# A feed forward in seven block products instead of eight, with its inner layer and the residual held in DRAM

## The chip, the core and the metric

The kernel runs on one core of one Trainium2 chip. The core has TensorE (PE) for matmuls, VectorE (DVE), ScalarE (ACT) and GpSimd (POOL) for element-wise work, and DMA queues that are fed in order by SyncE (SP) and a few other engines. The metric is the device time of one execution in microseconds, as the median of several runs.

## The reference

One decoder block on 1024 tokens of width 1024. What comes ahead of the feed forward (state-space and attention mixers, a gated merge, cross attention to 256 memory tokens) is left as it is. The last lines of the reference are these:

```
xo = memory_cross_attention(h, mem, w_xq[l], w_xkv[l], w_xo[l])
h = layer_norm(DEEPNORM_ALPHA * h + xo, ln2_g[l], ln2_b[l])

ff = jnp.square(jax.nn.relu(h @ w_ff1[l] + b_ff1[l])) @ w_ff2[l] + b_ff2[l]
h = layer_norm(DEEPNORM_ALPHA * h + ff, ln3_g[l], ln3_b[l])
```

The feed forward is 1024 x 1024 by 1024 x 4096, a squared ReLU, and 1024 x 4096 by 4096 x 1024.

## The kernel before

Every float32 product is made of three matmuls on rounded operands: each operand is split into a high part (a cast on ScalarE) and a low part (a subtraction on VectorE), and `mm3` (lines 99 to 102) sums high x high, high x low and low x high in one PSUM bank. A matmul covers 128 contraction rows, 128 stationary columns and 512 moving columns.

**Weights** come through the class `Stream` (lines 105 to 161). `load` starts a DMA on SP's queue into one of two raw buffers, `split` makes the two parts in one of `NWH` = 6 tile pairs (lines 136 and 137), `done` frees a pair. `pump` does one load and one split at each `slot()` (line 272); `slot` also runs deferred work (`defer`, line 269), whose count is in slots. All engines run their own instructions in the order in which the program writes them.

**The cross attention's last product** is a call of `nat_gemm` (line 1234 on) with `evac_xo` (lines 1324 to 1329): for each of two column halves it runs over eight token tiles `t` of 128; the last two tiles share their weight steps. After the second half, every pair of tiles gets its layer norm (`ln_pair`, line 1258 on): statistics on VectorE, the reciprocal root by small steps on GpSimd (`ln_rstd`, lines 212 to 233), the centering on VectorE (line 241), the scaling on ScalarE (line 250), the bias on GpSimd (line 252). Three slots later `tail_xo` transposes the tile on TensorE (line 262) and splits it into `xh` and `xl` (lines 255 and 256), which are the moving operand of the feed forward.

**The feed forward** (lines 1333 to 1397) goes over eight groups `hc` of 512 inner columns. For each it makes 2 halves of the tokens x 4 inner blocks x 8 contraction blocks x 3 matmuls (up), applies ReLU on ScalarE (line 1349), the square on GpSimd (1350), the split on ScalarE and VectorE (1351, 1352) into `fh`, `fl`; and then 8 token tiles x 2 column halves x 4 contraction blocks x 3 matmuls (down), whose PSUM result VectorE adds into the residual `hn` (line 1368). The inner layer stays in SBUF and never leaves it. In the last group the order is by token tile, so that the final layer norm of a pair can begin while later tiles are multiplied (lines 1369 to 1396); the last two tiles are normalized one by one on VectorE, and the last store follows line 1395. Other names that the change touches: `open_pool("ptp")`, the pools of temporaries `sgp` and `rows`, the layout of `wff2` in `_layout` (line 1458).

Of the kernel before, what the change touches and what calls it, by code (L numbers as in the profile page):

```python
# [10 lines left out]
FT = mybir.dt.float32  # L11
# [47 lines left out]
def block_kernel(ctx, tc, I, out, dbg=None):  # L59
# [45 lines left out]
    class Stream:  # L105
        def __init__(self):
            self.req = []
            self.key = {}
            self.nd = self.ns = self.nu = 0
            self.raw = {}  # L110
            self.sp = {}
            self.over = set()
            self.nstart = 0

# [4 lines left out]
        def load(self, limit=10 ** 9):  # L119
            while self.nd < min(len(self.req), limit) and self.nd - self.ns < (3 if self.nd < self.nstart else 2):  # L120
                ap, n = self.req[self.nd]
                if self.nd < self.nstart and self.nd % 3 == 2:
                    t = kvp.tile([128, 1024], FT, name="wrx", tag="wrx", bufs=1)
                else:
                    t = win.tile([128, 1024], FT, name="wraw", tag="wraw", bufs=2)
                sp.dma_start(t[:, :n], ap)
                self.raw[self.nd] = t
                self.nd += 1

        def split(self, limit=10 ** 9):  # L130
            while self.ns < min(self.nd, limit) and (self.ns < NWH or self.ns - NWH in self.over):
                n = self.req[self.ns][1]
# [3 lines left out]
                act.copy(h[:, :n], r[:, :n])  # L136
                dve.tensor_sub(l[:, :n], r[:, :n], h[:, :n].bitcast(FT))  # L137
# [18 lines left out]
        def done(self, key=None):  # L156
            i = self.nu if key is None else self.key[key]
# [12 lines left out]
    g_dr = dr.tile([16, 128, SEQ], FT, name="g_dr")  # L170

# [31 lines left out]
    for hc in range(8):  # L203
        for i in range(4):
            W.add(I["wff1"][4 * hc + i], 1024)
        for i in range(4):
            W.add(I["wff2"][4 * hc + i], 1024)

# [81 lines left out]
    hh = actp.tile([128, KB, SEQ], FR, name="acth", tag="acth")  # L290
    hl = actp.tile([128, KB, SEQ], FR, name="actl", tag="actl")
# [884 lines left out]
    mx_c, mx = open_pool("mx", "right")  # L1176
    xh = actp.tile([128, KB, SEQ], FR, name="acth", tag="acth")
    xl = actp.tile([128, KB, SEQ], FR, name="actl", tag="actl")
# [48 lines left out]
    def nat_gemm(ah, al, evac):  # L1227
        for c in range(2):
            for ts_ in [(t,) for t in range(NT - 2)] + [(NT - 2, NT - 1)]:
                ws = [[w.rearrange("p (k c) -> p k c", k=2) for w in W.get(i)] for i in range(4)]  # L1230
                ps_ = [mmbank() for _ in ts_]
                for i in range(4):
# [5 lines left out]
                    if len(ts_) > 1:  # L1238
                        W.done()
                        slot() if i == 1 else W.pump()  # L1240
# [3 lines left out]

    rows_c, rows = open_pool("rows", "right")
# [37 lines left out]
    ptp_c, ptp = open_pool("ptp", "right")  # L1283
    ph = ptp.tile([128, 4, SEQ], FR, name="ph")
    pl = ptp.tile([128, 4, SEQ], FR, name="pl")

    def evac_xs(c, t, p):
        pp = (sgp if t % 2 else ptp).tile([128, 512], FT, name="sg", tag="sg", bufs=2)
# [31 lines left out]

    def tail_xo(t):
        transpose_in(hn[:, t, :], xh, xl, t)

    def evac_xo(c, t, p):
# [3 lines left out]
        if c == 1 and t % 2:  # L1328
            ln_pair(t, g2_, b2_, tail_xo, 3, 3)

    nat_gemm(Cat(ph, xh), Cat(pl, xl), evac_xo)

# [1 line left out]
    fh, fl = ph, pl  # L1334
    for t in range(NT):
        defer(t, lambda t=t: dve.scalar_tensor_tensor(hn[:, t, :], hn[:, t, :], ALPHA, bf2, op0=OP.mult, op1=OP.add))
    for hc in range(8):
        if hc == 7:
            g3, b3 = load_rows("ln3_g", "ln3_b")
        for half in range(2):  # L1340
            s = slice(512 * half, 512 * half + 512)
            for i in range(4):
                w = [t.rearrange("p (k c) -> p k c", k=KB) for t in W.get(0 if half else i)]
                p = mmbank()
                for k in range(KB):
                    mm3(p, w[0][:, k, :], w[1][:, k, :], xh[:, k, s], xl[:, k, s], k == 0, k == KB - 1)
                r = sgp.tile([128, 512], FT, name="sg", tag="sg", bufs=2)
                j = COL_F1 + 4 * hc + i
                act.activation(r, p, AF.Relu, bias=cols[:, j:j + 1], scale=1.0)  # L1349
                pool.tensor_mul(r, r, r)  # L1350
                act.copy(fh[:, i, s], r)  # L1351
                dve.tensor_sub(fl[:, i, s], r, fh[:, i, s].bitcast(FT))  # L1352
                if half:
                    W.done()
                slot()
        last = hc == 7
        for c, t in [(c, t) for t in range(NT) for c in range(2)] if last else [(c, t) for c in range(2) for t in range(NT)]:
            cs = slice(512 * c, 512 * c + 512)
            p = mmbank()
            sl = slice(128 * t, 128 * t + 128)  # L1360
            ws = [[w.rearrange("p (k c) -> p k c", k=2) for w in W.get(2 * c * last + i)] for i in range(2)]
            for k in range(4):
                w = ws[k // 2]
                mm3(p, fh[:, k, sl], fl[:, k, sl], w[0][:, k % 2, :], w[1][:, k % 2, :], k == 0, k == 3)
                if t == NT - 1 and k % 2 and not last:
                    W.done()
                    W.pump()
            dve.tensor_add(hn[:, t, cs], hn[:, t, cs], p)  # L1368
            if last:
                x = hn[:, t, :]  # L1370
                ln_stats(lnst[:, t], x, (c,))
                def cen(h):
                    xx, gg = x[:, 512 * h:512 * h + 512], g3[:, 512 * h:512 * h + 512]
                    return lambda mv: dve.scalar_tensor_tensor(xx, xx, mv[:, 0, 0:1], gg, op0=OP.subtract, op1=OP.mult)

                if c == 1 and t % 2 and t < NT - 2:
                    xs = [hn[:, u, :] for u in (t - 1, t)]
                    w = ln_a(xs, [lnst[:, u] for u in (t - 1, t)], g3)

                    def fin(t=t, xs=xs, w=w):  # L1380
                        ln_b(xs, w, b3, (pool, pool))
                        for u, x in zip((t - 1, t), xs):
                            sp.dma_start(out[128 * u:128 * u + 128, :], x)

                    defer(1, fin)
                elif c == 1 and t == NT - 2:
                    mv, w = ln_rstd([lnst[:, t]], dve, [cen(0), cen(1)])
                    act.activation(x, x, AF.Copy, scale=w[:, 1, 0:1])
# [105 lines left out]
```

## Time and profile before

| | |
|---|---|
| median of 3 runs | 1945.02 us (1944.44 to 1945.78) |
| span of the profiled execution | 1943.7 us |
| feed forward, first to last matmul | 1221.0 to 1927.0 us of the span |
| PE, DVE, ACT, POOL busy | 97%, 50%, 29%, 31% of the span |
| mean granted TensorE clock | 0.990 |

The span runs from the first to the last instruction of one profiled execution; the times of the runs are a little longer. A busy TensorE is not by itself TensorE at its peak, since matmuls overlap: one record lasts 0.39 us, but the next starts 0.226 us after it. So stages are read by counts of matmuls in a stretch rather than by the sum of durations.

### The profile page before, as it was taken

How to read it: one execution, taken by the hardware profiler on the slowest of the kernel's cores; microseconds unless marked ns; L12 is line 12 of the kernel's file. 1: busy time of each engine (PE TensorE's matmuls, PEld its weight loads, DVE VectorE, ACT ScalarE, POOL GpSimd, SP SyncE). 2: the span in 40 equal slices, each digit the busy share in tenths (PEclk: the TensorE clock that was granted, in tenths of full speed). 3: DMA queues.
4: the chain of work that ended last, by engine and by line, in shares of the span. 5: the costliest groups of instructions: out<-in, count | busy, mean ns of one | idle time of the engine just before them, and what ended most of it. 6: DMA issues, size and time to landing. Idle time of an engine off the chain costs nothing.

```text
span 1943.7 us, 24170 instructions
## 1 busy us (share of the span) xinstructions
PE 1885.0 (97%) x9400; PEld 1619.6 (83%) x9400; DVE 966.7 (50%) x1678; ACT 563.7 (29%) x998; POOL 609.0 (31%) x782
## 2 busy tenths in 40 slices
PE   7899999999999998999999999999999999999996
PEld 7798788889999976788888888788888888888885
DVE  6526846675666666444556445542323223232328
ACT  4324343433332434322124322412121212213121
POOL 3305687474565335322034004401010100101016
PEclk9999999999999999999999999999999999999998
DMA  6545562130120243333511121111111111011102
GB/s 243 184 122 187 183 198 73 34 99 23 55 67 29 75 136 109 118 117 109 185 44 44 44 76 44 44 65 44 55 54 44 44 44 66 32 55 48 62 21 87
DMA packets 82563, 163.26 MB, mean 84 GB/s; under 512 B 19857, under 2 KB 39441, under 8 KB 82449
## 3 DMA queue, kind: packets, MB, share of 16 engines
q1 hardware_dynamic: 75968, 147.30, 22.8%
q10 hardware_dynamic: 5904, 12.85, 1.7%
q0 software_dynamic: 576, 1.57, 0.3%
q8 instruction: 74, 1.21, 0.3%
q14 instruction: 41, 0.33, 0.1%
HBM read 126.99 MB, written 34.70 MB: 83 GB/s over the span
## 4 chain that ended last, share of the span: by engine, by line
PE 86%; DVE 7%; ACT 2%; issue 2%; POOL 2%; DMA 1%; DVEq 0%; SPq 0%; ACTq 0%; POOLq 0%
PE mm L100 26%; PE mm L102 26%; PE mm L101 26%; PE ax L262 1%; DVE wlo L137 1%; PE ax L996 1%; PE ax L969 1%; PE ax L987 1%; PE ax L822 1%; ACT yh L1111 1%; PE ax L845 1%; PE ax L954 1%; PE ax L809 1%; DVE lnst L237 0%; PE ax L846 0%
## 5 line engine op out<-in xcount | busy, mean ns | idle before, releaser
L100 PE MATMUL mm<-acth,whi 128*128 128x512 f32 (+1 forms) x896 | 348.0, 388 | 4.9 <-ACT abst L611 4.6
L102 PE MATMUL mm<-acth,wlo 128*128 128x512 f32 (+1 forms) x896 | 345.5, 386 | 2.5 <-DVE wlo L137 2.5
L101 PE MATMUL mm<-actl,whi 128*128 128x512 f32 (+1 forms) x896 | 345.4, 386 | 0.3 <-DVE actl L256 0.3
L136 ACT CAST whi<-wraw 128x1024 fp32r<-128x1024 f32 (+1 forms) x169 | 168.4, 996 | 419.5 <-PE mm L102 300.9
L137 DVE TENSOR_TENSOR wlo<-wraw,whi 128x1024 fp32r<-128x1024 f32 (+1 forms) x169 | 213.2, 1263 | 146.9 <-ACT whi L136 144.6
L100 PE MATMUL mm<-whi,acth 128*128 128x512 f32 (+1 forms) x704 | 281.7, 400 | 0.0
L102 PE MATMUL mm<-whi,actl 128*128 128x512 f32 (+1 forms) x704 | 270.7, 384 | 0.0
L101 PE MATMUL mm<-wlo,acth 128*128 128x512 f32 (+1 forms) x704 | 270.4, 384 | 0.0
L1350 POOL TENSOR_TENSOR sg<-sg 128x512 f32<-128x512 f32 x64 | 67.8, 1059 | 574.4 <-ACT sg L1349 574.4
L100 PE MATMUL mm<-whi,ph 128*128 128x512 f32 x576 | 224.3, 389 | 0.0
L102 PE MATMUL mm<-whi,pl 128*128 128x512 f32 x576 | 224.1, 389 | 0.0
L101 PE MATMUL mm<-wlo,ph 128*128 128x512 f32 x576 | 224.1, 389 | 0.0
L100 PEld LDWEIGHTS mm<-acth,whi 128*128 128x128 f32 x896 | 171.1, 191 | 38.4 <-ACT abst L611 5.5
L102 PEld LDWEIGHTS mm<-acth,wlo 128*128 128x128 f32 x896 | 170.6, 190 | 36.4 <-DVE wlo L137 3.0
L101 PEld LDWEIGHTS mm<-actl,whi 128*128 128x128 f32 x896 | 171.1, 191 | 32.6 <-DVE actl L256 0.5
L102 PEld LDWEIGHTS mm<-whi,actl 128*128 128x128 f32 x704 | 168.0, 239 | 15.3
L101 PEld LDWEIGHTS mm<-wlo,acth 128*128 128x128 f32 x704 | 168.6, 239 | 14.2
L100 PEld LDWEIGHTS mm<-whi,acth 128*128 128x128 f32 x704 | 167.5, 238 | 15.4
L1352 DVE TENSOR_TENSOR pl<-sg,ph 128x512 fp32r<-128x512 f32 x64 | 44.3, 692 | 261.8 <-ACT ph L1351 261.8
L1368 DVE TENSOR_TENSOR hn<-hn,mm 128x512 f32<-128x512 f32 x128 | 87.0, 685 | 163.7 <-PE mm L102 163.7
L102 PEld LDWEIGHTS mm<-whi,pl 128*128 128x128 f32 x576 | 108.1, 188 | 22.4
L101 PEld LDWEIGHTS mm<-wlo,ph 128*128 128x128 f32 x576 | 108.1, 188 | 22.4
(322 smaller groups left out, 2882.6 us busy)
## 6 DMA issues: line engine op xcount, KB each, us to landing
wraw<-in_wff_dram SPq DMA_DIRECT2D x64, 512.0 KB
wraw<-in_wg_dram SPq DMA_DIRECT2D x16, 512.0 KB
gl<-g_dr SPq DMA_DIRECT2D x32, 256.0 KB
wraw<-in_wqk_dram SPq DMA_DIRECT2D x12, 512.0 KB
wraw<-in_wglu_dram SPq DMA_DIRECT2D x16, 384.0 KB
g_dr<-abst SPq DMA_DIRECT2D x16, 256.0 KB
a_dr<-abst ACTq DMA_DIRECT2D x16, 256.0 KB
b_dr<-abst ACTq DMA_DIRECT2D x16, 256.0 KB
```

Source lines behind the costliest of these rows:

```text
L100: pe.matmul(o, lhsT=lh, rhs=rh, start=first, stop=False)
L101: pe.matmul(o, lhsT=lh, rhs=rl, start=False, stop=False)
L102: pe.matmul(o, lhsT=ll, rhs=rh, start=False, stop=last)
L136: act.copy(h[:, :n], r[:, :n])
L137: dve.tensor_sub(l[:, :n], r[:, :n], h[:, :n].bitcast(FT))
L262: pe.transpose(p[:, k, :], x[:, (4 * b + k) * 128:(4 * b + k + 1) * 128], ident)
L809: pe.matmul(p[:, g, :], lhsT=xe[:, g].rearrange("p j o -> p (j o)"), rhs=d["cm"][:, g, 0:8, :].rearrange("p j o -> p (j o)"), start=True, ...
L822: pe.matmul(p[:, g, :], lhsT=d["bt"][:, g, :], rhs=d["U"][:, g, :], start=True, stop=True)
L845: pe.matmul(p[:, g, :], lhsT=dts[:, g, :], rhs=d["U"][:, g, :], start=True, stop=False)
L1350: pool.tensor_mul(r, r, r)
L1352: dve.tensor_sub(fl[:, i, s], r, fh[:, i, s].bitcast(FT))
L1368: dve.tensor_add(hn[:, t, cs], hn[:, t, cs], p)
```

## The change

The whole feed forward is replaced. Both products are cut into 2 x 2 blocks (tokens 0 to 511 and 512 to 1023; contraction halves; column pairs), and each 2 x 2 block product is made from seven block products of sums and differences instead of eight plain ones.

- **Operands from the activations.** The tails of the cross attention's layer norm (`tail_lo`, `tail_hi`) make, besides the transposed blocks, three combined blocks S1, S2 and A11 - A21, and later S4 (`s4h`, `s4l`). `keep_residual` stores alpha * h + bias to a DRAM tensor `h2_dr`. The last two token tiles are normalized singly on VectorE.
- **Operands from the weights.** `operand` casts and subtracts one block for a product and then forms the next difference in place on GpSimd. For the up product it fills half of a stream tile (`f1_fill`), for the down product a whole 2048-column pair (`f2_weights`).
- **The up product** goes over 16 steps `j` of two inner blocks; `f1_step` combines the seven PSUM results on VectorE into four blocks, applies ReLU and square on ScalarE, forms sums and differences on GpSimd and stores seven tiles to `f_dr` in DRAM by SP's queue.
- **The down product** goes over four blocks `c` of 1024 inner columns and seven products each; the stationary operands are read back from `f_dr` by the weight stream, the residual from `h2_dr`. Products "1" and "6" are collected in `a1` and `a6` and added to the output by GpSimd in the last block; results "5" and "7" are added twice, once by VectorE and once through ScalarE and GpSimd. The final layer norm follows inside the last block (`last_pair`, `last_one`).

Cut to its core:

```
+    def tail_hi(t):
+        u = t - 4
+        cs = slice(128 * u, 128 * u + 128)
+        ct = slice(512 + 128 * u, 640 + 128 * u)
+        p = turned(t)
+        a11, a12 = flat(hn[:, u, 0:512]), flat(hn[:, u, 512:1024])
+        sa, s1 = flat(tmp(0)), flat(tmp(1))
+        act.copy(sa, p[0])
+        dve.tensor_add(s1, p[1], sa)
+        s2 = flat(tmp(0))
+        pool.tensor_sub(s2, s1, a11)
+        split_ps(xh[:, 0:4, ct], xl[:, 0:4, ct], s1)
+        split_ps(xh[:, 4:8, ct], xl[:, 4:8, ct], p[1])
+        pool.tensor_sub(sa, a11, sa)
+        split_ps(ph[:, :, cs], pl[:, :, cs], s2)
+        pool.tensor_sub(a12, a12, s2)
+        split_ps(ph[:, :, ct], pl[:, :, ct], sa)
+        keep_residual(t)
...
+    def operand(q, b11, b21, b12, b22, h, l):
+        src = {"1": b11, "2": b21, "3": b22, "4": b21, "5": b11, "6": b22, "7": b12}[q]
+        act.copy(h, src)
+        dve.tensor_sub(l, src, h.bitcast(FT))
+        if q == "1":
+            pool.tensor_sub(b11, b12, b11)
+        elif q == "3":
+            pool.tensor_sub(b12, b22, b12)
+            pool.tensor_sub(b22, b22, b11)
+        elif q == "6":
+            pool.tensor_sub(b21, b21, b22)
...
+    f1_seq = [(j, q) for j in range(16) for q in ("1267543" if j < 15 else "1567243")]
...
+    t_free = [(ph[:, :, 0:512], pl[:, :, 0:512]), (ph[:, :, 512:], pl[:, :, 512:]),
+              (quad(xh, 1, 0), quad(xl, 1, 0)), (quad(xh, 1, 1), quad(xl, 1, 1))]
+    f2_order = ["1", "2", "6", "5", "3", "7", "4"]
+    f2_made = ["1", "2", "3", "6", "5", "7", "4"]
...
+        if q == "1":
+            act.copy(u, p)
+        elif q == "2":
+            dve.tensor_add(x11, u, p)
+            relu2(x11, x11, 2 * j)
+            put(1, x11)
...
+        elif q == "4":
+            dve.tensor_add(x21, x21, p)
+            relu2(x21, x21, 2 * j)
+            pool.tensor_add(s1, x21, x22)
+            pool.tensor_sub(s2, s1, x11)
+            pool.tensor_sub(x21, x11, x21)
+            put(5, s1)
+            put(6, s2)
+            put(7, x21)
...
+    f1_step(0, "1")
+    f1_step(0, "2")
+    while later:
+        slot()
...
+            def second(x):
                 r = sgp.tile([128, 512], FT, name="sg", tag="sg", bufs=2)
+                act.copy(r, p)
+                pool.tensor_add(x, x, r)
+
+            if q in "16":
+                a = (a1 if q == "1" else a6)[:, t, :]
+                add(a) if c else act.copy(a, p)
+                if done:
+                    for x in (c11, c12, c21, c22) if q == "1" else (c12, c21, c22):
+                        pool.tensor_add(x, x, a)
...
+            if t == 0:
+                f2_weights(n + 2)
```

`done` is true in the last column block (c = 3). `f2_weights(n + 2)` makes the operand that stands two places later in `f2_made`; since "6" and "5" come earlier in `f2_order`, these are made one product ahead of their use.

## Rows read from the trace of the kernel before

**Rows 1.** The page's head and its busy times: us, share of span, instructions.
```profile
span 1943.7 us, 24170 instructions
PE 1885.0 (97%) x9400; PEld 1619.6 (83%) x9400; DVE 966.7 (50%) x1678; ACT 563.7 (29%) x998; POOL 609.0 (31%) x782
```

**Rows 2.** Busy us (instructions) per engine in stretches; then clock, DMA share, GB/s.
```profile
1221.00:1927.00 706.00, 701.78 (x3105) 581.10 (x3103) 245.08 (x316) 155.28 (x203) 104.14 (x121) 1.00 0.14 48
1927.00:1943.70 16.70, 0.32 (x2) 0.00 (x0) 12.73 (x29) 1.26 (x2) 6.42 (x3) 0.61 0.32 126
1300.00:1500.00 200.00, 200.00 (x884) 165.62 (x883) 59.13 (x73) 40.39 (x52) 17.68 (x17) 1.00 0.15 50
```

**Rows 3.** Timeline of PE at the feed forward's start: start, duration, operation, [idle before].
```profile
1238.44 0.39 PE L100 MATMUL mm<-acth,whi 128*128 128x512 f32 x1
1242.29 1.09 PE L262 MATMUL ax<-cst,hn 128*128 128x128 f32 x8 [3.01 <-POOL hn L252]
1244.60 1.97 PE L262 MATMUL ax<-cst,hn 128*128 128x128 f32 x8 [1.21 <-POOL hn L252]
...
1246.79 0.63 PE L101 MATMUL mm<-actl,whi 128*128 128x512 f32 x1
1247.22 0.63 PE L102 MATMUL mm<-acth,wlo 128*128 128x512 f32 x1
1247.65 0.56 PE L100 MATMUL mm<-acth,whi 128*128 128x512 f32 x1
```

**Rows 4.** Timelines of the end: DVE's last operation, then SP's last store.
```profile
1939.07 1.42 DVE L1395 SCALAR_TENSOR_TENSOR hn<-hn,rs,row 128x512 f32<-128x512 f32 x2
...
1939.85 0.33 SPq L1396 DMA_DIRECT2D out_dram<-hn  x1
```

**Rows 5.** VectorE's groups by shape, 1300 to 1880: busy us, mean ns, idle before.
```profile
L1368 DVE TENSOR_TENSOR hn<-hn,mm 128x512 f32<-128x512 f32 x103 | 70.1, 685 | 146.7 <-PE mm L102 146.7
L137 DVE TENSOR_TENSOR wlo<-wraw,whi 128x1024 fp32r<-128x1024 f32 x52 | 63.7, 1226 | 31.4 <-ACT whi L136 29.6
L1352 DVE TENSOR_TENSOR pl<-sg,ph 128x512 fp32r<-128x512 f32 x54 | 37.4, 692 | 230.1 <-ACT ph L1351 230.1
```

**Rows 6.** ScalarE's groups by shape, 1300 to 1880.
```profile
L136 ACT CAST whi<-wraw 128x1024 fp32r<-128x1024 f32 x52 | 54.6, 1051 | 241.3 <-PE mm L102 241.3
L1349 ACT ACTIVATE sg<-mm,cols 128x512 f32<-128x512 f32 x55 | 38.0, 690 | 154.6 <-PE mm L102 154.6
L1351 ACT CAST ph<-sg 128x512 fp32r<-128x512 f32 x54 | 33.5, 621 | 62.1 <-POOL sg L1350 62.1
```

**Rows 7.** GpSimd: two lines of code (min/median/max ns), then a group (mean ns).
```profile
L1350 POOL TENSOR_TENSOR sg<-sg x64: 1037/1040/2091, 1234.1 to 1884.6; 128x512 f32<-128x512 f32 x64
...
L252 POOL TENSOR_TENSOR hn<-hn,row x22: 2331/2402/3388, 1002.9 to 1928.8; 128x1024 f32<-128x1024 f32 x22
...
L1204 POOL TENSOR_TENSOR sb<-sb,gl 128x512 f32<-128x512 f32 x16 | 25.6, 1602 | 50.7 <-DVE sb L375 50.7
```

**Rows 8.** DMA, 0 to 200 us, in 40 slices of 5 us.
```profile
GB/s 184 400 414 408 324 16 174 141 204 206 300 277 307 104 189 153 104 55 55 243 19 177 179 120 77 80 162 37 202 155 187 302 239 107 265 205 134 135 108 179
```

**Rows 9.** Timelines of DVE and POOL: layer norm of tiles 6 and 7.
```profile
1225.57 0.68 DVE L1326 SCALAR_TENSOR_TENSOR hn<-hn,mm 128x512 f32<-128x512 f32 x1
...
1228.85 2.47 DVE L241 SCALAR_TENSOR_TENSOR hn<-hn,bmv,row 128x1024 f32<-128x1024 f32 x2
...
1238.86 5.68 POOL L252 TENSOR_TENSOR hn<-hn,row 128x1024 f32<-128x1024 f32 x2 [3.72 <-ACT hn L250]
```

**Rows 10.** Timelines of POOL and DVE near the end, the same stretch.
```profile
1924.13 0.19 POOL L224 TENSOR_TENSOR rs<-rs 128x2 f32<-128x2 f32 x1
1924.41 0.19 POOL L229 TENSOR_SCALAR rs<-rs 128x2 f32<-128x2 f32 x1
...
1926.14 4.94 POOL L252 TENSOR_TENSOR hn<-hn,row 128x1024 f32<-128x1024 f32 x2 [1.26 <-ACT hn L250]
...
1926.49 2.31 DVE L223 TENSOR_TENSOR rs<-rs 128x1 f32<-128x1 f32 x1
1928.84 2.26 DVE L224 TENSOR_TENSOR rs<-rs 128x1 f32<-128x1 f32 x1
```

**Rows 11.** VectorE by line of code: duration in ns, min/median/max.
```profile
L1368 DVE TENSOR_TENSOR hn<-hn,mm x128: 669/686/689, 1280.3 to 1933.8; 128x512 f32<-128x512 f32 x128
...
L223 DVE TENSOR_TENSOR rs<-rs x6: 148/154/2315, 1925.4 to 1938.3; 128x1 f32<-128x1 f32 x6
```

More of the change, by code (lines that the diff above doesn't have):

```diff
@@ L202, in block_kernel @@
         W.add(b_dr[i].rearrange("p a c -> p (a c)"), 1024)
[L203 to L207, printed above, removed]
+    W_FF = len(W.req)
     stp = con
@@ L1280, in block_kernel @@
     nat_gemm(xh, xl, evac_mix)
[L1283 to L1285 removed]
     def evac_xs(c, t, p):
[L1288 removed]
+        pp = (sgp if t % 2 else rows).tile([128, 512], FT, name="sg", tag="sg", bufs=2)
         pv = p.rearrange("p (h m) -> p h m", h=2)
@@ L1327, in evac_xo @@
         ln_stats(lnst[:, t], hn[:, t, :], (c,))
[L1328 to L1341, printed above, removed]
-            for i in range(4):
[L1343 to L1346, printed above, removed]
-                r = sgp.tile([128, 512], FT, name="sg", tag="sg", bufs=2)
[L1348 to L1388, printed above, removed]
-                    pool.tensor_add(x, x, b3)
-                    sp.dma_start(out[128 * t:128 * t + 128, :], x)
-                elif c == 1 and t == NT - 1:
-                    mv, w = ln_rstd([lnst[:, t]], dve, [cen(0), cen(1)])
-                    for h in range(2):
-                        ss = slice(512 * h, 512 * h + 512)
-                        dve.scalar_tensor_tensor(x[:, ss], x[:, ss], w[:, 1, 0:1], b3[:, ss], op0=OP.mult, op1=OP.add)
-                        (act if h else sp).dma_start(out[128 * t:128 * t + 128, ss], x[:, ss])
@@ new lines, in block_kernel, with f1_fill, fill @@
+    f1_at = {(j, q): 7 * j + n for j in range(16) for n, q in enumerate(f1_made)}
+    f1_seq = [(j, q) for j in range(16) for q in ("1267543" if j < 15 else "1567243")]
+    def f1_fill(m):
+        def fill(h, l):
+            for i in range(2):
+                j, n = divmod(2 * m + i, 7)
+                operand(f1_made[n], *raws[j], half(h, i), half(l, i))
+                if n == 6:
+                    raw_load(j + 2)
+        return fill
+    for m in range(56):
+        W.add(f1_fill(m), (lambda: raw_load(0)) if m == 0 else None)
@@ new lines, in block_kernel, with f1_product @@
+    nat_gemm(Cat(ph, xh), Cat(pl, xl), evac_xo, True)
+    fs = None
+    stage = [None, None]
+    f1_left = {m: 2 for m in range(56)}
+    def f1_product(j, q, p):
+        m, i = divmod(f1_at[j, q], 2)
+        h, l = (half(a, i).rearrange("p (k c) -> p k c", k=4) for a in W.at(W_FF + m))
+        sh, sl_ = A7[q]
+        for k in range(4):
+            mm3(p, h[:, k, :], l[:, k, :], sh[:, k], sl_[:, k], k == 0, k == 3)
+        f1_left[m] -= 1
+        if not f1_left[m]:
+            W.done(at=W_FF + m)
```

279 lines of the change are left out of this document (262 added, 17 removed).

## Prediction

> **What bounds the kernel now.** I read the page's busy shares first: TensorE works 97% of the span, every other engine at most half of it [rows 1]. The table by stretch then shows where the change lies: from the first feed-forward matmul (1221.0 us) to the last (1927.0) there are 706.0 us, and inside them, in 1300 to 1500, TensorE is busy 200.00 of 200 us at granted clock 1.00 with 884 matmuls [rows 2]. So one 128x512 matmul costs 200/884 = 0.2263 us, and a matmul that disappears there gives that back, unless something else comes late. The stage has 3072 of them (8 groups x (8x24 + 16x12)): 695.2 us. The other 10.8 us lie at its start: TensorE pauses 3.01 and 1.21 us for the last layer norm's tokens, makes 32 transposes, and restarts at half clock (0.43 us spacing, the 1.2 GHz level against 2.4) [rows 3]. Behind the last matmul the final layer norm and store take 1943.7 - 1927 = 16.7 us [rows 2, 4]. The profiled span is 1943.7; the median of the runs is 1945.0, so I add 1.3 to every span.
>
> **What is removed.** Seven block products replace eight: up product 16 x 7 x 12 = 1344 matmuls, down product 28 x 48 = 1344, together 2688. 384 x 0.2263 = **-86.9 us**. All remain 128x512 with a fresh stationary tile each, the form measured, so I take the same pitch. The squares move from GpSimd to ScalarE, which has room.
>
> **The up product in its steady part.** A j lasts 7 x 12 x 0.2263 = 19.0 us. VectorE has 7 adds from PSUM (0.685) and 7 subtractions for the low halves (0.692): 9.6 us [rows 5]. ScalarE has one copy, 8 activations and 7 casts at 0.62 to 0.69: 10.5 us [rows 6]. GpSimd has 8 additions of 512 columns at 1.04: 8.3 us [rows 7]. All fit, operands are made up to six tiles ahead, and eight PSUM banks give a product 21 us of grace: 0 us. The new traffic is seven 256 KB stores and 1 MB of weights per j, 150 GB/s, where the first 200 us of the trace moved up to 414 GB/s in a slice [rows 8]. SP carries it all in order: a store that waits for its squares holds the weight loads behind it, but these are wanted a j (19 us) later. If that cover failed, one held load of a few us per j would cost 16 x 3 = 48 us; I take 0.
>
> **The start of the up product is dearer.** Before, four column blocks of 24 matmuls on the first 512 tokens (21.7 us) covered the last layer norm, and still TensorE paused. Now only products "1" and "2" (24 matmuls, 5.4 us) can run before "6", which needs the combined blocks of all tokens. The chain behind the last cross-attention matmul runs through VectorE's queue in program order: tails of tiles 2 and 3 (8 operations), one weight fill (2), the layer norm of tile 7 (5, and 2.3 us of tiny ones), tails of tiles 4 to 6 (21: each has the sum, four low halves, two residual operations), the add of "2" (1), and 4 of tile 7's. 41 x 0.68 = 27.9, + 2.3 = 30.2 us without any wait. Each tail also hops between ScalarE, VectorE and GpSimd three times, its temporaries wait for the residual's store to DRAM, and GpSimd's two 1024-wide additions for tiles 4 and 5 (2.4 each, [rows 7]) fall into the same time. No row shows such a tail; from below they cost 0, from above 10 us. The nearest row is the old pair of tiles 6 and 7, which went from first VectorE operation at 1225.57 to GpSimd's last addition at 1244.5, though VectorE's own share was under 7 us [rows 9]; so waits are real and I take 5. "6" starts about 35 us behind, of which 5.4 are matmuls: 29.6 lost against 10.8, **+19**, and 1.5 for a longer restart at half clock [rows 3]: **+20** (14 to 28).
>
> **Turn from up to down.** 4 MB of raw down weights are fetched behind product "5" of the last j; five products (13.6 us) and "1" of the down product (10.9) run meanwhile, and "2" needs the last megabyte. At 300 to 400 GB/s [rows 8] they land after 10 to 14 us, plus ScalarE 2.1 and VectorE 2.45 (two 1024-wide operations each, [rows 5, 6]). **+1** (0 to 4). The reload of the residual is wanted a product later: 0.
>
> **The down product, first three column blocks.** A product is 48 x 0.2263 = 10.86 us. VectorE: 4 adds, two 1024-wide and one 2048-wide low halves, 2.74 + 2.45 + 2.45 = 7.6. A GpSimd operation over 2048 columns is in no row: four times the 512 row gives 4.2, twice the slowest 1024 row 6.8, and I take 4.5, near the plain 1024 rows doubled (4.7) [rows 7]. Per block it has four of these and eight 512 adds, 26.4 of 76 us. What makes it tight is that the two engines exclude each other: two tiny VectorE multiplies, normally 0.16 us, took 2.31 and 2.26, until each of GpSimd's two additions ended [rows 10, 11]. But 128 VectorE adds that read PSUM stayed within 669 to 689 ns [rows 11]. So only VectorE's 4.9 us with two SBUF inputs collide. Operand "6" needs three GpSimd subtractions in a row, yet they run ahead; I find it ready about 0.5 us early. **+2** for all three blocks (0 to 6).
>
> The Trainium skill (SBUF — State Buffer, "SBUF: two separate sides") calls this port pair an exclusive lock, held for the whole instruction, taken by GpSimd operations and by VectorE operations with two SBUF inputs. By that rule the collisions below are all paid; without it the last block would end some 20 us earlier, which is the first rival.
>
> **The last column block** is the other dear place. There the kept products "1" and "6" are added into the output by GpSimd: 16 and 12 adds, and 8 for "5" and "7". GpSimd's list: 36 x 1.05 = 37.8; subtractions for "3" and "6" 3 x 4.5 = 13.5; three pair layer norms, 12 tiny steps each at 0.27, 9.9 [rows 10]; seven 1024-wide additions, 16.5 [rows 7]. 77.7 us, for seven products of 76.0. Into the same time fall VectorE's excluding operations: 8 x 1.23, 4 x 2.45 and six centerings of 1.24 [rows 5, 9]: 27.0. Since GpSimd has work queued throughout, they add: 105. It can begin only 3.6 us into the block (12 matmuls and an add); gaps where it waits for ScalarE's scaling I put at 6; the last tile's normalization and store after it at 4. 3.6 + 105 + 6 + 4 = 118.6 us, against 76.0 + 16.7 = 92.7: **+26**. TensorE itself waits some 5 us for operand "6" of this block and 3 for "5", but that is inside. From below, if exclusion costs nothing and the gaps close: 3.6 + 77.7 + 4 = 85, and the old tail rules with a denser end: +8. From above, adds at 1.60 (the row of an addition under contention) [rows 7] and longer gaps: +40.
>
> The Trainium skill (GPSIMD Engine Reference, "Engine selection") speaks against this placing: elementwise additions belong on VectorE, GpSimd being about twice as slow. The rows say 1.04 against 0.69, one and a half. By the page's factor the 36 adds would be an estimated 49 instead of 37.8 us and the kernel end 11 us later, about 1919.
>
> **Sum.** -86.9 + 20 + 1 + 2 + 26 = -38; 1943.7 - 38 = 1906, + 1.3: **1907 us**. With all lower ends -86.9 + 14 + 8 = -65 (1880); with all upper ends -86.9 + 28 + 4 + 6 + 40 = -9 (1936).
>
> **Rivals.** *Nearly all is kept.* VectorE's operations slip between GpSimd's and the last block ends like before (+8 or less), and the tails overlap better (+8): -71, 1874. For it: VectorE is busy only 50% and GpSimd 31% over the span [rows 1], and only few rows show the exclusion. Against it: in the last block GpSimd's own list already exceeds the products. Chance 0.14.
>
> *Slower: the down product becomes VectorE's.* One mechanism, in all 28 products: VectorE needs 7.6 us of a product's 10.86, and if it also stands through GpSimd's 3.8 us per product, 11.4, with ScalarE's cast ahead of every low half and the next product's operand made only one product ahead, TensorE waits for operands each time. It decides from a pitch of 10.86 + 38/28 = 12.2 us per product; at 13.5 the kernel would be 28 x 2.64 = 74 us later than forecast, 1981. For it: two thirds of VectorE is taken. Against it: the weight tiles are three products deep, and the PSUM banks give a whole product of slack. Chance 0.12.
>
> *A queue holds it:* SP's order delays weight loads (16 x 3 us as above), 1955 with the rest; chance 0.04. That fewer matmuls would not shorten the stage is excluded: its steady part has no other wait than TensorE.
>
> **How the numbers follow.** My forecast (1880 to 1936) has 0.70, the rivals 0.14, 0.12 and 0.04. About 0.2%, 4 us, is what a measurement can tell from no change. Faster by more: the forecast, the first rival, less what ends close to the old time: 0.82; same 0.05; slower 0.13. The range leaves out the rivals' outer parts: 1874 to 1945.
>
> **What would show it.** 2688 matmuls at 0.226 us; "6" starting 30 to 40 us behind the last cross-attention matmul, with VectorE full in between; no waits of TensorE through the up product; in the last block GpSimd busy without a break and TensorE done 25 to 40 us before the end. I am wrong if TensorE waits in the up product or in every down product, or if the end follows the last matmul by 17 us.

## The result, and the profile after

The changed kernel takes **1992.9 us** (median of 4; 1992.4 to 1994.4) against 1945.4 (1944.4 to 1945.8): 1.0243 times the time before, 95% interval 1.0228 to 1.0257. The forecast was 1907, and 1945 was its upper bound; the kernel became slower by 47.5 us instead of faster by 38. The profiled span went from 1943.7 [rows 1] to 1991.4.

Head and busy times of the page of after (us, share of the span, instructions):

```profile
span 1991.4 us, 24693 instructions
PE 1826.8 (92%) x9016; PEld 1559.3 (78%) x9016; DVE 1239.2 (62%) x1884; ACT 712.1 (36%) x1212; POOL 915.5 (46%) x922
```

Against [rows 1] the 384 matmuls are gone (9400 to 9016). VectorE has 272 us more work, GpSimd 306 and ScalarE 148. TensorE's share fell from 97 to 92%: it waits now.

The table by stretch of after, cut at the last cross-attention matmul, product "6" of the first step, the last up matmul, the first down matmul, the last column block and the last matmul (columns as in [rows 2]):

```profile
1222.70:1273.20 50.50, 13.90 (x57) 10.70 (x56) 37.71 (x57) 22.77 (x38) 23.51 (x15) 0.64 0.15 57
1273.20:1595.50 322.30, 309.09 (x1320) 248.57 (x1320) 199.97 (x221) 146.54 (x247) 178.63 (x122) 0.99 0.40 142
1595.50:1604.80 9.30, 0.14 (x1) 0.00 (x0) 4.04 (x6) 4.49 (x5) 0.00 (x0) 0.68 0.81 291
1604.80:1863.50 258.70, 239.44 (x1014) 195.80 (x1015) 195.24 (x143) 106.83 (x104) 109.98 (x41) 0.95 0.49 168
1863.50:1951.40 87.90, 78.25 (x329) 63.07 (x328) 58.58 (x57) 21.50 (x19) 73.58 (x48) 0.96 0.19 60
1951.40:1991.40 40.00, 0.94 (x5) 0.43 (x3) 29.67 (x55) 7.54 (x9) 27.73 (x35) 0.57 0.27 105
```

At the old pitch of 0.2263 us per matmul each stretch has an ideal, and the excess is the bill. Two cuts of the rows above are a little off: the last block's first matmul starts at 1862.3 and the last matmul of all ends at 1952.3, so the table takes the last block from 1862.3.

| stretch | measured | ideal | excess | forecast |
|---|---|---|---|---|
| start to "6" | 50.5, and 1.7 begun later | 5.4 of matmuls, and the 10.8 lost before | +36 | +20 |
| up product from "6" | 322.3 | 110 products x 2.716 = 298.7 | +23.6 | 0 |
| turn | 9.3 | 0 | +9.3 | +1 |
| down, blocks 0 to 2 | 257.5 | 21 x 10.86 = 228.1 | +29.4 | +2 |
| last block to the end | 129.1 | 76.0 + 16.7 | +36.4 | +26 |

With -86.9 for the matmuls the sum is +47.8; the spans differ by 47.7. No term is missing, and all five were too small. Where TensorE ran, the pitch stood: the up product's clock was 0.99. In the down product it was 0.95, since TensorE comes back from each long wait at the lower of its two levels (granted clock 0.50, that is 1.2 GHz, in 1605 to 1612, behind waits of 9.19 and 1.53 us). In blocks 0 to 2, 41 matmuls that did not wait start later than the pitch behind such waits, together by 8.0 us.

### The profile page after: what moved, and what is told of

Its sections match the earlier page's. It is cut to its first block, busy times and chain, and to the rows that moved or that the text cites. A ratio compares the mean times of both kernels' runs of the same rounds, so it can differ in the third digit from the quotient of the medians.

```text
span 1991.4 us, 24693 instructions
## 1 busy us (share of the span) xinstructions
PE 1826.8 (92%) x9016; PEld 1559.3 (78%) x9016; DVE 1239.2 (62%) x1884; ACT 712.1 (36%) x1212; POOL 915.5 (46%) x922
## 5 line engine op out<-in xcount | busy, mean ns | idle before, releaser
L159 DVE TENSOR_TENSOR wlo<-wraw,whi 128x1024 fp32r<-128x1024 f32 (+1 forms) x161 | 244.2, 1528 | 154.5 <-ACT whi L158 153.2
L100 PE MATMUL mm<-acth,whi 128*128 128x512 f32 (+1 forms) x576 | 225.9, 392 | 10.5 <-ACT abst L633 5.1
L101 PE MATMUL mm<-actl,whi 128*128 128x512 f32 (+1 forms) x576 | 223.8, 389 | 7.1 <-DVE actl L1447 6.8
L102 PE MATMUL mm<-acth,wlo 128*128 128x512 f32 (+1 forms) x576 | 223.4, 388 | 7.4 <-DVE wlo L1447 4.8
L100 PE MATMUL ax<-acth,whi 128*128 128x512 f32 x288 | 115.6, 401 | 17.0 <-ACT acth L1446 8.7
L1447 DVE TENSOR_TENSOR wlo<-wraw,whi 128x512 fp32r<-128x512 f32 x56 | 69.6, 1275 | 91.1 <-ACT whi L1446 91.1
L101 PE MATMUL ax<-actl,whi 128*128 128x512 f32 x288 | 115.1, 400 | 5.3 <-DVE actl L1447 5.3
L102 PE MATMUL ax<-acth,wlo 128*128 128x512 f32 x288 | 114.5, 397 | 1.3 <-DVE wlo L1447 1.3
L100 PE MATMUL mm<-ph,whi 128*128 128x512 f32 x224 | 87.7, 392 | 3.5 <-DVE hn L1547 3.5
L101 PE MATMUL mm<-pl,whi 128*128 128x512 f32 x224 | 87.2, 389 | 0.0
L102 PE MATMUL mm<-ph,wlo 128*128 128x512 f32 x224 | 87.2, 389 | 0.0
```

Of the source, the lines that this page charges most:

```text
L100: pe.matmul(o, lhsT=lh, rhs=rh, start=first, stop=False)
L101: pe.matmul(o, lhsT=lh, rhs=rl, start=False, stop=False)
L102: pe.matmul(o, lhsT=ll, rhs=rh, start=False, stop=last)
L1447: dve.tensor_sub(l, src, h.bitcast(FT))
```

## Where the waits come from

**GpSimd's addition was mis-sized.** Groups of after by shape (busy us, mean ns; idle before):

```profile
L1667 POOL TENSOR_TENSOR hn<-hn,a 128x512 f32<-128x512 f32 x28 | 48.1, 1753 | 7.5 <-DVE a L1655 7.5
L1660 POOL TENSOR_TENSOR hn<-hn,sg 128x512 f32<-128x512 f32 x32 | 46.9, 1477 | 118.9 <-ACT sg L1659 118.9
L1452 POOL TENSOR_TENSOR w2raw<-w2raw 128x2048 f32<-128x2048 f32 x4 | 18.4, 4601 | 18.5 <-DVE actl L1447 9.2 <-DVE pl L1447 9.2
L1447 DVE TENSOR_TENSOR wlo<-wraw,whi 128x512 fp32r<-128x512 f32 x56 | 69.6, 1275 | 91.1 <-ACT whi L1446 91.1
L1655 DVE TENSOR_TENSOR hn<-hn,ax 128x512 f32<-128x512 f32 x40 | 26.5, 678 | 5.5 <-POOL hn L1667 5.3
```

The additions that I put at 1.05 us take 1.48 and 1.75 in the mean, and 1.27 to 1.30 undisturbed; the means hold the time in which VectorE shuts GpSimd out. The row of 1.04 [rows 7] multiplied one tensor by itself; the last row of that group, which reads two tensors and which I kept for the upper bound, was the right model (its median is 1.29 us, its mean 1.60). My 4.5 us for 2048 columns was right (4.60). The Trainium skill (GPSIMD Engine Reference, "Engine selection") had GpSimd at about twice VectorE's time; 1.29 against 0.68 agrees, and my ratio of one and a half was wrong.

VectorE's subtraction with two SBUF inputs has a mean of 1.275 us in this group where 0.69 was measured [rows 5]; its additions from PSUM stay at 0.678. So the exclusion of [rows 10, 11] acts in the up product too, though not everywhere: the same subtraction from the blocks kept in `hn` (40 of them) has a median of 0.68.

**The up product** has no engine that is full, and TensorE waits three times in every two steps. Timelines of after: TensorE's matmuls that waited (1355 to 1399), then ScalarE and GpSimd in the same stretch:

```profile
1356.14 0.47 PE L100 MATMUL mm<-ph,whi 128*128 128x512 f32 x1 [0.56 <-DVE hn L1547]
1362.11 0.51 PE L100 MATMUL mm<-acth,whi 128*128 128x512 f32 x1 [0.24 <-ACT whi L1446]
1363.60 0.50 PE L102 MATMUL mm<-acth,wlo 128*128 128x512 f32 x1 [0.76 <-DVE wlo L1447]
1396.67 0.47 PE L100 MATMUL mm<-ph,whi 128*128 128x512 f32 x1 [0.59 <-DVE hn L1547]
...
1380.76 1.12 ACT L1446 CAST whi<-wraw 128x512 fp32r<-128x512 f32 x2
...
1390.19 0.62 ACT L1446 CAST whi<-wraw 128x512 fp32r<-128x512 f32 x1 [7.31 <-POOL wraw L1452]
...
1379.65 1.29 POOL L1558 TENSOR_TENSOR hn<-hn 128x512 f32<-128x512 f32 x1 [7.12 <-ACT hn L1519]
...
1383.99 1.73 POOL L1568 TENSOR_TENSOR sg<-hn 128x512 f32<-128x512 f32 x1
1385.69 1.74 POOL L1449 TENSOR_TENSOR wraw<-wraw 128x512 f32<-128x512 f32 x1
...
1388.87 1.29 POOL L1452 TENSOR_TENSOR wraw<-wraw 128x512 f32<-128x512 f32 x1
```

GpSimd stands 7.12 us for ScalarE's square (L1519), makes four block sums (6 us), and only then the next weight differences. The first of these overwrites the block of product "1", so it has to wait for that block's cast (ScalarE, 1380.76) and subtraction (VectorE, three of them from 1381.40 in 4.88 us); it could have begun at about 1383 and began at 1385.69. ScalarE stands 7.31 us for the third of these with its next activations behind it. The weights' cover of six tiles is gone each time: from 1356.14 to 1396.67 two steps take 40.5 us instead of 38.0. This pattern makes 15.3 of the stage's 23.6 us; 4.8 lie in its last step (waits of 1.32 and 1.28 us for weights, which no run here took away) and 2.7 in the restart behind "6".

**The turn and the first block.** Timelines of after at the turn: SyncE's queue, ScalarE, TensorE (its last two lines are operand "6" of blocks 1 and 2):

```profile
1590.18 6.54 SPq L145 DMA_DIRECT2D wraw<-f_dr  x3
1596.81 2.76 SPq L1487 DMA_DIRECT2D w2raw<-in_wff_dram  x4
1599.79 23.37 SPq L1530 DMA_DIRECT2D f_dr<-hn  x7
1623.25 0.87 SPq L145 DMA_DIRECT2D wraw<-f_dr  x2
...
1594.06 1.05 ACT L158 CAST whi<-wraw 128x1024 fp32r<-128x1024 f32 x1 [7.88 <-DMA wraw<-f_dr]
...
1627.26 1.05 ACT L158 CAST whi<-wraw 128x1024 fp32r<-128x1024 f32 x1 [10.41 <-DMA wraw<-f_dr]
...
1604.83 0.80 PE L100 MATMUL ax<-ph,whi 128*128 128x512 f32 x1 [9.19 <-ACT ph L1446]
...
1640.15 0.80 PE L100 MATMUL ax<-acth,whi 128*128 128x512 f32 x1 [8.69 <-ACT acth L1446]
...
1724.62 0.50 PE L101 MATMUL mm<-actl,whi 128*128 128x512 f32 x1 [3.71 <-DVE actl L1447]
1806.38 0.50 PE L101 MATMUL ax<-actl,whi 128*128 128x512 f32 x1 [3.69 <-DVE actl L1447]
```

The 4 MB of raw down weights are issued at 1596.81, behind the down product's own first tiles, instead of right behind product "5"; and seven stores hold SyncE's queue for 23 us, with the next tiles behind them. ScalarE stands twice for such a tile.

**The end.** GpSimd, then VectorE, at the end of after:

```profile
1885.42 21.00 POOL L1667 TENSOR_TENSOR hn<-hn,a 128x512 f32<-128x512 f32 x12
1906.38 4.60 POOL L1454 TENSOR_TENSOR w2raw<-w2raw 128x2048 f32<-128x2048 f32 x1
1910.94 19.02 POOL L1667 TENSOR_TENSOR hn<-hn,a 128x512 f32<-128x512 f32 x12
...
1966.07 0.69 DVE L1655 TENSOR_TENSOR hn<-hn,mm 128x512 f32<-128x512 f32 x1 [4.50 <-POOL hn L1660]
...
1982.02 2.26 DVE L249 SCALAR_TENSOR_TENSOR rs<-rs 128x1 f32<-128x1 f32 x1
```

GpSimd works from 1885 to 1934 without a break. The second of VectorE's last four additions runs 13.7 us behind the end of the last matmul: GpSimd's addition to the same block stood behind its bias additions.

## The experiments

Times are of single executions beside one of before (1946.0 to 1947.3) unless a median is named; twelve executions of before in one batch lay between 1942.3 and 1948.7, so differences under 3 us are read from traces only. "Less" is against 1992.9. Part of a difference can lie ahead of the change: the last cross-attention matmul starts at 1222.5 in the trace of after, but 2.3 us sooner in that of the first run below, and 4.6, 3.7, 1.8 and 3.8 us sooner in those of the next four. What these edits gained behind that matmul is so much less.

**Up product's weight differences on VectorE.**

```
-operand(f1_made[n], *raws[j], half(h, i), half(l, i))          # in operand(): pool.tensor_sub
+operand(f1_made[n], *raws[j], half(h, i), half(l, i), dve)     # in operand(): e.tensor_sub
```

> The up product's weight differences (four of 512 columns in each of 16 steps) go from GpSimd to VectorE; nothing else changes. The changed kernel has 1993 us, and its up product loses about 2.5 us in every two steps. GpSimd theory (a difference that stands in GpSimd's queue behind the block sums holds ScalarE's next cast, and with it ScalarE's and VectorE's queues): two steps fall from 40.5 us to 38.0 to 38.6, the kernel by 14 to 20 us, to 1973 to 1979. Rival, VectorE's load: it gets 2.8 us per step on top of 9.6 of 19.0, the waits stay or grow, 1990 to 2000. Rival, late weights from DRAM: no change, 1993.

Measured 1983.4, 9.5 less, between the two forecasts. The wait of TensorE that is left:

```profile
1359.60 0.50 PE L102 MATMUL mm<-acth,wlo 128*128 128x512 f32 x1 [0.55 <-DVE wlo L1447]
```

It recurs at 1398.50, so two steps take 38.9 us; of the three waits one is left. The up product is 10.0 us shorter, but the wait at the turn grows from 9.2 to 11.2. So GpSimd's order of work caused about two thirds of the steady loss (1.6 of each 2.5 us); VectorE, which got the work, did not become late. The edit changes the price of a difference too, but that is not the gain: from the start of the first to the end of the third they took 4.5 us on GpSimd and 5.3 in VectorE's list.

**Down product's weight differences on VectorE** (the same edit in `f2_weights`).

> The down product's weight differences (four of 2048 columns per column block) go from GpSimd to VectorE. GpSimd theory: the waits for operand 6 (8.9 and 2.2 us in the first block, 3.9, 3.8 and 5.8 in the others, with the slower clock behind each some 30 us) all but go, and the list in the last block loses 14 us: 20 to 35 us, 1958 to 1973. Rival, queue order at the turn (loads of the inner layer wait on SP behind stores of late sums): the first block's wait stays, only 10 to 18 us go, 1975 to 1983. Rival, VectorE's load: at 8.9 of 10.86 us per product it falls behind, 1993 or more.

Measured 1972.3, 20.6 less. The waits of 3.71 and 3.69 us in blocks 1 and 2 are gone; 7.6 us at the first "6" and 11.6 at the turn stay, as the queue-order rival said. Without the 4.6 us ahead of the change the gain is 16, in that rival's range. This also tells against my slower rival: VectorE got 16 operations of 2.3 us more, and the kernel became faster.

**The last block's 28 additions on VectorE.**

```
-                        pool.tensor_add(x, x, a)
+                        dve.tensor_add(x, x, a)
```

> The 28 additions of products 1 and 6 into the output go from GpSimd to VectorE (28 x 0.69 = 19 us there instead of 48 on GpSimd). GpSimd theory: the end follows the last matmul by 18 to 25 us instead of 40, and the wait for operand 6 of the last block goes: 20 to 30 us, 1963 to 1973. Rival, VectorE's load: VectorE is as full as GpSimd in that block, it only changes places, 1985 to 1997.

Measured 1986.2, 6.7 less, 3.7 of it ahead of the change; the rival was right. VectorE and GpSimd in the last block of this run:

```profile
1873.55 10.86 DVE L1667 TENSOR_TENSOR hn<-hn,a 128x512 f32<-128x512 f32 x4
...
1885.04 1.29 DVE L1667 TENSOR_TENSOR hn<-hn,a 128x512 f32<-128x512 f32 x2
...
1873.06 4.60 POOL L1452 TENSOR_TENSOR w2raw<-w2raw 128x2048 f32<-128x2048 f32 x1 [11.69 <-DVE pl L1447]
1877.74 4.91 POOL L1454 TENSOR_TENSOR w2raw<-w2raw 128x2048 f32<-128x2048 f32 x1
```

Four additions took 10.86 us, where two undisturbed ones take 1.29 in the same list: VectorE stands while each of GpSimd's operations runs. Operand "6" is then late by 15 us (TensorE's wait at 1896.51). Moving part of the work to the faster engine gained little here, while the other still worked on SBUF. The Trainium skill (SBUF — State Buffer, "SBUF: two separate sides") has the pair of ports locked for a whole instruction, which these rows bear out.

**The stream's weight filled one tile later at the start** (`W.cap = W_FF + 2`).

> One line: the stream may run ahead by two tiles instead of three until the up product starts, so the third weight fill (operands 7 and 5) is no longer written ahead of tile 7's layer norm. Queue-order theory: VectorE begins that layer norm 6 to 10 us sooner and product 6 starts 6 to 10 us sooner (50.5 us behind the last cross-attention matmul becomes 41 to 45): 1983 to 1987. GpSimd theory: the chain of tails is bound by the hops through GpSimd and the fill comes later anyhow: less than 3 us, 1990 to 1994.

Measured 1989.3, 3.6 less. "6" starts 47.4 us behind the start of the last cross-attention matmul instead of 50.7, and new waits of 3.2 us for the next weights (2.31 and 0.92) take that back; 1.8 of the 3.6 us lie ahead of the change (that matmul at 1220.7 instead of 1222.5). The fill was a small part of the start.

**The three together.**

> All weight differences of both products on VectorE, and the third weight fill held back (the edits of e1, e2 and e4 together). If the three losses are separate places: 9.6 + 20.7 + 3.6 less than 1993, 1959 (1955 to 1963). If VectorE's load begins to count when it takes all: 1965 to 1980. The waits at the turn (11 us) and for operand 6 of the first column block (8 us) should stay, since by the queue-order theory they come from SP's order and not from GpSimd's differences.

Measured 1961.6, 31.3 less, near the sum of 33.7. The waits at the turn (10.2 us) and for operand "6" of the first block (9.4) stayed, as expected. TensorE's waits lie one behind the other, so what each edit removes adds up.

**The tails' three differences on VectorE, with the late fill.**

> The three differences in each of the four upper tails go from GpSimd to VectorE, and the third weight fill is held back as in e4 (1989). GpSimd theory: a tail takes 5 to 6.5 us of VectorE's queue instead of 7.1 to 10.3, product 6 starts 6 to 12 us sooner than in e4: 1977 to 1983. VectorE's load: twelve operations of 0.69 us more on the engine whose queue is the chain: 1988 to 1996.

Measured 1988.2, the rival's time: "6" comes 44.0 us behind that matmul instead of 47.4, and the turn's wait is 12.9 us instead of 9.4 in the run with the late fill alone. What the start gained was lost at the turn.

**The first raw down weights on ScalarE's queue.**

> The four first loads of the down weights (4 MB) are issued from ScalarE's queue instead of SP's, where they stand behind loads of the inner layer that wait for a raw buffer. Queue-order theory: they start 8 to 12 us sooner, the wait of 9 us at the turn goes to 0 to 3, and part of the 9 us for operand 6 of the first block: 1980 to 1986. Rival, DRAM bandwidth (about 390 GB/s while they run): they only compete earlier with the same traffic, 1990 to 1995.

Measured 1991.7: nothing. ScalarE issued them at 1594.2, only 2.6 us sooner, since it stood itself at the cast that waits 7.96 us for a stored tile. TensorE's waits fell to 6.1 us at the turn and to 5.2 at the first "6", but the matmul behind that one waited 4.8 us instead of 1.6. A queue of an engine that waits is no shorter way.

**12 fewer additions** (product "1" is added into the kept "6" first, both then go out in one addition).

```
+                    if q == "6":
+                        dve.tensor_add(a, a, a1[:, t, :])
-                    for x in (c11, c12, c21, c22) if q == "1" else (c12, c21, c22):
+                    for x in (c11,) if q == "1" else (c12, c21, c22):
```

> In the last column block product 1's sum is added into product 6's on VectorE (4 operations), so that GpSimd makes 16 additions instead of 28; the numbers computed are the same. GpSimd's list as the bound of the last block: 12 x 1.29 to 1.75 = 15 to 21 us less there, the kernel 12 to 18 us sooner, 1975 to 1981, the end following the last matmul by 25 to 32 us. Rival, the final normalization's own chain bounds the end: less than 5 us, 1988 to 1993.

Measured 1984.4, 8.5 less. TensorE's waits in the block are mostly gone, but the end is still 38 us behind the last matmul: there VectorE waits 4.49 us for GpSimd's addition as before.

**And the second targets added from PSUM by VectorE** (in the last block `second = add`).

> In the last column block the second target of products 5 and 7 is added by VectorE from PSUM (8 additions of 0.69 us) in place of ScalarE's copy and GpSimd's addition, and product 1 is added into the held product 6 first, so that GpSimd has 8 additions fewer there (second targets) and 12 fewer for products 1 and 6 (16 in place of 28). Theory: the end, 40.0 us behind the last matmul, is long because the additions of the last products wait in GpSimd's queue behind the 28 additions and the bias additions; then the tail falls to 20 to 26 us and the time to 1964 to 1974 us. Rival: the end is set by GpSimd's pair norms and bias additions themselves and by the port that VectorE shares with them; then the tail stays over 33 us and the time is 1979 to 1985 us, as with the fewer additions alone (1984.4).

Measured 1974.6, 18.3 less, at the edge of the theory; the tail of 29.6 us lies in neither range. The tail, by stretch:

```profile
1943.10:1972.70 29.60, 0.13 (x1) 0.00 (x0) 25.19 (x51) 5.42 (x5) 16.80 (x20) 0.58 0.27 106
```

From the end of the last matmul the tail was 16.4 us before, 39.1 after and is 29.5 here: 9.6 of the 22.7 us that it had grown by were the additions in GpSimd's queue. The other 13 are put down to VectorE's list by its busy time, 25.19 us in 51 instructions (some stretched beside GpSimd's bias additions) against 12.73 in 29 [rows 2]: one product now finishes four row tiles, and their layer norms all come at the end. No run here changes that list.

**The order of transfers at the turn.** Two tiles instead of four are split before the up product's end, the raw weights are issued ahead of the other two, and the last step's four late stores behind them.

```
+            if j == 15 and n in (3, 5, 6, 7):
+                late_puts.append(...)
...
-    W.cap = 10 ** 9
+    W.cap = W.scap = W_FF + 58     # scap limits what is split
```

> Only the order of the transfers at the turn from up to down product is changed: two tiles of the stored inner layer are loaded and split before the up product's end in place of four, the loads of the down product's first raw weights are issued ahead of the third and fourth of them, and the last step's four stores of GpSimd-made sums are issued behind the first product's first loads. Theory: the wait at the turn (9.2 us) and much of that for the first product 6 (8.85 and what lies around it, 13 us) come of SyncE's queue order and of a ScalarE cast that stands for its tile; then the turn's wait is under 3 us, that of the first product 6 under 6, and the time 1974 to 1982 us. Rival: the first product 6 waits for GpSimd's differences of 4.6 us each, and what is saved at the turn is lost there: 1984 to 1990 us. If the transfers that now come together slow each other, no gain: 1990 to 1995 us.

Measured 1992.1, no gain. TensorE at the turn and at the first "6":

```profile
1597.87 0.49 PE L100 MATMUL ax<-ph,whi 128*128 128x512 f32 x1 [2.61 <-ACT ph L1446]
1638.34 0.80 PE L100 MATMUL ax<-acth,whi 128*128 128x512 f32 x1 [12.90 <-ACT acth L1446]
```

The turn's wait fell from 9.2 to 2.6 us, and that of the first "6" grew from 8.7 to 12.9; the rest went in small waits and restarts behind them. The queue held the turn, but the time was passed on, to a chain that the order of transfers does not touch.

**All of it together**, in executions repeated in turn with before:

> Weight differences of both products on VectorE, the stream's weight filled later at the start, the last block's direct additions and the new order at the turn, together. Theory: the losses lie one behind the other on the matmul engine, so the gains add: 1961.6 us (differences and late fill) less 16 to 24 for the last block and less 10 to 18 for the turn gives 1920 to 1936 us, below the kernel before (1945). Rival: VectorE, which now takes the differences and the additions, becomes late in the last block and at the turn, and half of the gains are lost again: 1938 to 1950 us.

Median 1949.6 against 1945.5 (ratio 1.0018, 1.0008 to 1.0028); the rival's time, and its reason at the turn (in the last block no wait of over 1 us was left). 10.6 us of wait remained at the first "6" and 5.5 at the second product. VectorE and TensorE there:

```profile
1600.11 3.39 DVE L1447 TENSOR_TENSOR actl<-w2raw,acth 128x2048 fp32r<-128x2048 f32 x1
1603.42 2.28 DVE L1451 TENSOR_TENSOR w2raw<-w2raw 128x2048 f32<-128x2048 f32 x1
1605.73 2.29 DVE L1452 TENSOR_TENSOR w2raw<-w2raw 128x2048 f32<-128x2048 f32 x1
1607.95 2.35 DVE L159 TENSOR_TENSOR wlo<-wraw,whi 128x1024 fp32r<-128x1024 f32 x2
...
1609.22 0.79 PE L102 MATMUL mm<-ph,wlo 128*128 128x512 f32 x1 [5.55 <-DVE wlo L159]
1631.88 0.79 PE L100 MATMUL ax<-acth,whi 128*128 128x512 f32 x1 [10.57 <-ACT acth L1446]
```

The split of the second product's tiles (L159) stands behind operand "3", whose differences "6" wants two products after "1", and whose own product comes four after it; the tiles' buffers come free that much later, ScalarE stands for the next loads, and the cast for "6" behind it.

**The third and fourth operands made behind those splits**, both within the first product.

```
-                f2_weights(n + 2)
+                if n > 1:
+                    f2_weights(n + 2)
...
+            if n == 0 and t in (0, 2):
+                f2_weights(2 + t // 2)
```

> The combination of before (differences on VectorE, late fill, direct additions in the last block, order of the turn's transfers) with the down product's third and fourth operands made while its first product runs, behind the splits of that product's stream tiles instead of ahead of them. Theory: what is left at the turn (5.7 us in the second product for a split that stands behind four 2048-column operations on VectorE, 10.7 + 2.1 us for operand 6 whose cast stands on ScalarE behind casts that wait for their tiles) is order within the queues alone; then 13 to 18 us go and the time is 1932 to 1937 us, below the kernel before. Rival: the stream's two buffers and the transfers' latency pace it; then the waits only change places and it is 1944 to 1950 us.

Median 1939.4 against 1946.0: ratio **0.9963** (0.9948 to 0.9977). The wait for "6" is gone, that of the second product (5.2) stays: the theory's cause, with 10 of its 13 to 18 us.

**The start: row tiles 4 and 5 scaled one slot earlier, products "1" and "2" behind the tails.**

> As the run with the new order of operands, and at the start the scaling and bias additions of rows 4 and 5 are issued one slot earlier, and the first two up products are issued behind the last four tails in place of between them. Theory: operand 6 comes some 45 us behind the last matmul of the cross attention because VectorE and ScalarE stand in other work's order (additions that lock them, the first products' evacuations between the tails); then it comes 8 to 12 us sooner and the time is 8 to 12 us below that run. Rival: the four tails' own chain across four engines paces it, 7 to 10 us each; then under 4 us are gained.

Measured 1939.7, no gain. "6" starts 45.3 us behind the last cross-attention matmul, 47.4 in the run before; the rival (under 4 us) was right.

**And the tails' differences on VectorE.**

> As the run with the new start, and the tails' three differences on VectorE. Theory: with the turn in order VectorE's longer queue has no further wait to cause, and the tails run back to back (6.2 us each): another 3 to 6 us. Rival: as in the single run of that edit, what is gained at the start is lost at the turn: 0 to 1 us.

Median **1934.5** against 1946.0: ratio **0.9941** (0.9927 to 0.9956), 2.9% below the change as made and 0.6% below the kernel before. The same edit that gained nothing alone gains some 5 us here: "6" starts 42.1 us behind that matmul, 3.2 sooner than in the run before, as it had started 3.4 sooner alone, but the turn's wait stays at 2.2 us (2.1 in the run before), so nothing later gives it back. Its stretches, cut like those of after:

```profile
1221.30:1263.20 41.90, 16.05 (x57) 11.81 (x56) 36.95 (x63) 18.41 (x32) 7.95 (x4) 0.63 0.17 63
1263.20:1578.20 315.00, 307.13 (x1320) 250.96 (x1320) 226.31 (x291) 150.61 (x255) 90.79 (x60) 0.98 0.42 147
1578.20:1903.60 325.40, 312.88 (x1345) 256.42 (x1344) 260.01 (x233) 129.11 (x120) 82.55 (x68) 0.97 0.47 160
1903.60:1933.50 29.90, 0.15 (x1) 0.00 (x0) 25.19 (x51) 5.41 (x5) 16.78 (x20) 0.59 0.27 105
```

By the ledger above: start +26, up product +16, turn and down product +21, end +13, against -87: -10, as measured. At the start VectorE is busy 37 of 42 us, so what is left there is its own work. Of the up product's +16, 9 us are waits and slow matmuls just behind "6" and 5 lie in the last step; the steady steps in between lose only 2.

## Why the prediction was wrong, step by step

- **-86.9 for the matmuls** held: 384 fewer, the same pitch. That the stage gives back a matmul's time "unless something else comes late" held too; nearly everything came late.
- **The up product at 0** is the first step that failed. I summed each engine's busy time per step, found 8 to 10 us of 19, and took the rest for room. The order inside the queues decides: GpSimd, late from its wait for a square, made the block sums ahead of the weight differences that ScalarE and the weights waited for. The price that I named for lost cover (a held load) was of another mechanism, with the wrong engine. +23.6, of which 15.3 are this pattern; with the differences on VectorE two thirds of each loss went.
- **The start at +20.** The mechanism was right, VectorE's queue; both of its terms were mis-sized, about equally. The 30.2 us of work were 37.7 busy in the row of after, with the exclusion in it; the 5 us for waits were 12.8. VectorE stood for ScalarE, tile 7's layer norm behind a weight fill, and the tails for their temporaries' stores (GpSimd waited 3.4 us for one, twice).
- **The turn at +1** failed in its first clause: "fetched behind product '5'" was read from the code's order, and the queue had other loads and stores ahead. +9.3.
- **The first three blocks at +2.** The step "they run ahead; I find it ready about 0.5 us early" failed. Of +29.4, 13.1 are waits in the first block, 11.0 of them at "6", which went only when the order of the operands was changed as well as that of the transfers (5.2 at the second product came in their place); 7.7 are GpSimd's differences in blocks 1 and 2; 8.0 are the lower clock behind the waits, which I had priced at the start alone.
- **The last block at +26** had the right mechanism and sign; 118.6 was forecast, 129.1 measured. GpSimd was busy for 101.3 us of it (73.58 + 27.73, exclusion included), near the 105 of the sum, but by luck: its list at undisturbed prices (1.29 for an addition, 4.6 for a subtraction) is 87 us and not 77.7, which leaves some 15 us for the exclusion and not 27. The mis-sized term is the time in which GpSimd does nothing, 3.6 + 6 + 4 = 13.6 us forecast and 27.8 measured. That the four layer norms are VectorE's at the end was in no step; by the busy times that is some 13 us.
- **The rivals.** "Slower" decided from 12.2 us per product, and the mean pitch was 12.4 (346.6 us for 28), but not by its mechanism: the waits lie at ten places, and more work on VectorE made the kernel faster. SyncE's queue, put at 3 us in each step and chance 0.04, was real only at the turn.

All five terms left out the same thing, the time in which an engine stands with other work queued behind it; three of them I took at or near their lower ends. They are not independent, so they were not wrong in both directions but all in one, and the range was too narrow by what [rows 9] had shown once: 7 us of work spread over 19.

What stays open: why two tiles' split at the second down product still costs 5 us, why the up product's last step loses some 5 us in every run, and what of the start an order with fewer operations per tail would save; none of these was tried.

## What to carry to other kernels

When work moves to helper engines, write down each helper's instruction list in issue order with what each waits for, not the sum of its durations; a wait in the middle is paid by all that is queued behind it. Take an operation's price from a row with the same number of different operands, and count the time of two engines that exclude each other together, as an upper bound (here some 15 of 27 us were added to GpSimd's time). An edit that removes one of several waits in a chain may show no gain until the next one is gone too, so test such edits on top of each other as well as alone.

## What the runs showed of the hardware

- GpSimd multiplied a 512-column tensor by itself in 1.04 us and added two different ones in 1.27 to 1.30; 2048 columns took 4.6. VectorE needed 0.68 and 2.29.
- With GpSimd at work on SBUF, VectorE operations with two SBUF inputs took up to several times their time (four additions 10.86 us, where two undisturbed ones took 1.29), and GpSimd's own additions rose from 1.29 to 1.75 in the mean; VectorE's additions from PSUM stayed at 0.68.
- Behind each long wait TensorE ran at the lower of its two levels for a while (granted clock 0.50 in 1605 to 1612): 8.0 us in all in 1604.8 to 1862.3, a second price of a wait.
